# Second layer's heads: transposes of two units in a row in every other step

## The chip, the cores and the metric

The kernel runs on one core of a Trainium2 chip. The time is the device time of one execution in microseconds (us), the median of several runs. One execution is also recorded by the hardware profiler, and the profile shows that one alone.

The engines of a core work side by side, each through its own list of instructions in order: TensorE (PE for matmuls, PEld for its weight loads), VectorE (DVE), ScalarE (ACT), GpSimd (POOL), and SyncE (SP), which issues most DMAs here. An instruction that needs another engine's result waits for a semaphore, and everything behind it on its engine waits too.

## What is computed

Two layers of a bidirectional encoder over 512 tokens of width 1024, in float32. The first layer mixes tokens by neighbourhood attention, the second by multi-head latent attention; after each comes a gated embedding and at the end an RMSNorm. The change is in the second layer's heads:

```python
def block_attention(q, k, v):
    ...
    def one(qblk):
        s = jnp.einsum('bqhd,bkhd->bhqk', qblk, k).astype(jnp.float32) * scale
        pr = jax.nn.softmax(s, axis=-1).astype(v.dtype)
        return jnp.einsum('bhqk,bkhd->bqhd', pr, v)
    o = lax.map(one, qb)
    ...

def mixer_mla(xn, w_in, q_norm, w_qb, kv_norm, w_kvb, w_out):
    ...
    o = block_attention(q, k, v)
    return (o.reshape(B, S, H * MLA_V) * jax.nn.silu(z)) @ w_out
```

There are 16 heads and 512 queries, so 4 blocks of 128 queries for each head. Queries and keys have 64 plain and 32 rotary columns, and are projected from low-rank vectors.

## The kernel before

A float32 operand is kept as two float32r tiles, hi and lo (hi a rounded copy, which ScalarE writes, lo the rest, which VectorE or GpSimd subtracts), and a product of two operands is three matmuls: hi by hi, lo by hi, hi by lo. Weights come in by DMA as `wraw`, and `load_w` (L83, L84) splits them into `wwhi` on ScalarE and `wwlo` on GpSimd, here in two pieces each. What TensorE leaves in PSUM is evacuated by `split` (L94 on ScalarE, L96 or L98 on VectorE).

`mla_heads` works on 64 **units**: unit u is query block u mod 4 of head u // 4. A unit goes through three functions:

- `score(u)`: three matmuls of 512 columns into a PSUM tile `ps_S` (there are two of them), then the softmax by rows: VectorE takes the maximum (mx, L844), ScalarE the exponential with its row sum (L846), VectorE the reciprocal (rc, L847), and GpSimd multiplies (L848). The result is the tile `ex`, of which there are four.
- `turn(u)`: four transposes of 128x128 on TensorE (L139) of `ex` into a PSUM tile `ps_T` (there are three), which `split` evacuates to the head's tiles `pt_hi` (ScalarE, L94) and `pt_lo` (VectorE, L96).
- `output(h, s)`: for a whole head, four matmuls with `pt_hi` (s = 0) or `pt_lo` (s = 1) into the one PSUM tile `ps_O` (L863). Then `half_of` takes the result out (L204, L205), and after every second head `gated` multiplies by the gate and splits (L209 and L213 on GpSimd, L212 on ScalarE).

Beside them run the `pieces`: projections of the next heads' queries, keys and values (L751, L107), cut into parts over eight steps, with their weight loads. In every second group of eight steps a `rope` piece ends: ScalarE copies it (L784), VectorE shuffles and multiplies (L785, L786), GpSimd multiplies by the sine and adds (L787, L788), ScalarE and GpSimd split it (L789, L790). In steps 48 to 67 TensorE also works on pieces of the embedding (`ple`).

A loop of 70 steps lays this out. Step i holds, in this order, `score(i)`, the pieces of that step, a `turn`, and in steps with i mod 4 of 0 or 1 an `output` of the head two before. `turn` lags by three steps: unit i - 3 in step i. Each function is issued after the last matmul so far (`issue_after`), so TensorE's order is that of the loop. On the other engines a scheduler sets the order when the program is built, from its own modelled timeline; so a change of the loop changes the order of ScalarE, VectorE and GpSimd as well, though the loop says nothing of them.

Of the kernel before, what the change touches and what calls it, by code (L numbers as in the profile page):

```python
# [40 lines left out]
class Trunk:  # L41
# [692 lines left out]
    def mla_heads(self, pool, xT, cT, sets, oT):  # L734
# [98 lines left out]
        def score(i):  # L833
            h, qt = i // 4, i % 4
            st = sets[h // 2 % 2]
            q, k, kk = ((st["qe"], st["ke"], 96), (st["qo"], st["ko"], 128))[h % 2]
            if qt == 0:
                ST[h] = [self.small.tile([P, 4], F32, name=n, tag=n) for n in ("mx", "sm", "rc")]
            mx, sm, rc = (t[:, qt:qt + 1] for t in ST[h])
            sp = self.psum("S")  # L840
            Q = lambda s: q[s][0:kk, qt * P:(qt + 1) * P]
            K = lambda s: k[s][0:kk, :]
            self.mms(sp, [(Q(0), K(0)), (Q(0), K(1)), (Q(1), K(0))])
            nc.vector.reduce_max(mx, sp, axis=AX.X, negate=True)  # L844
            ex = EX[i] = pool.tile([P, S], F32, name="ex", tag="ex", bufs=4)
            nc.scalar.activation(ex, sp, AF.Exp, bias=mx, accum_out=sm)  # L846
            nc.vector.reciprocal(rc, sm)  # L847
            nc.gpsimd.tensor_tensor(out=ex, in0=ex, in1=rc.to_broadcast([P, S]), op=ALU.mult)  # L848

        def turn(i):  # L850
            h, qt = i // 4, i % 4
            if qt == 0:
                PT[h] = self.bigtile("pt_hi"), self.bigtile("pt_lo")
            ex = EX.pop(i)
            t = self.transposes([ex[:, n * P:(n + 1) * P] for n in range(4)])
            self.split(*(x[:, :, qt * P:(qt + 1) * P] for x in PT[h]), t.rearrange("p (a b) -> p a b", a=4))

        def output(h, s):
            if s == 0:
                PS["o", h] = self.psum("O")  # L860
            O = PS["o", h]
            for kt in range(4):
                self.last_mm = nc.tensor.matmul(O, V[h // 4][kt][:, h % 4 * P:(h % 4 + 1) * P], PT[h][s][:, kt, :],  # L863
                                                start=s == 0 and kt == 0, stop=s == 1 and kt == 3)
            if s == 0:
                return
            j, e = h // 2, h % 2
            if e == 0:
                U[j] = pool.tile([P, S], F32, name="u", tag="u", bufs=2)
            self.half_of(U[j], O, e)  # L870
            if e == 1:
                self.gated(U[j], zs[j], oT, j)

        def pieces(j):

            n, g = j + 1, j // 2 + 1
            w = [[] for i in range(8)]
            add = lambda i, f, *x: w[i].append(lambda: f(*x))
            if j == 0:
                add(0, queries, n, 0, 4)  # L880
                add(1, queries, n, 4, 9)
                add(2, keys, n, 0, 5)
                add(3, keys, n, 5, 6)
                for t in range(NT):
                    add((3, 4, 4, 5)[t], values, 0, t, "OOTT"[t])
            elif j < 7:
                add(0, queries, n, 0, 1)
                add(1, queries, n, 1, 3)
                add(2, queries, n, 3, 9)
                add(3, keys, n, 0, 4)  # L890
                add(4, keys, n, 4, 6)
            if j % 2 == 0 and j < 6:
                add(4, load_qn, g, ("k", n))
                add(5, rope, g, 0, 1)
                add(6, rope, g, 1, 5)
                add(7, rope, g, 5, 9)
                add(7, load_kv, g, ("r", g))
            elif j == 6:
                add(4, load, "w0", a["proj"][1, 0], 1024, ("q", n))
                add(6, ple)  # L900
                add(7, ple)
            elif j < 7:
                add(2, *((load_qr, g + 1, ("q", n), ("rl", g)) if j < 5 else
                         (load, "p", a["pT"][1], 1024, ("q", n), ("rl", g))))
                for t in range(NT):
                    add(6 + t // 2, values, g, t)
            else:
                add(0, load, "w1", a["proj"][1, 1], 1024, "latest")
                for i in (0, 1, 2, 3, 3, 4, 5, 6, 7, 7):
                    add(i, ple)  # L910
            return w
# [32 lines left out]
        for i in range(70):  # L944
            work = []
            if i < 64:
                work.append(lambda: score(i))
                work += pieces(i // 8)[i % 8]
            elif i < 68:
                work.append(ple)  # L950
            if 3 <= i < 67:
                work.append(lambda: turn(i - 3))
            if i >= 8 and i % 4 < 2:
                work.append(lambda: output(i // 4 - 2, i % 4))
            for f in work:
                with self.tc.issue_after(self.last_mm.ins):
                    f()
            if i == 53:
                last = self.last_mm
# [296 lines left out]
```

## Time and profile before

| what | value |
|---|---|
| median of 3 runs | 657.49 us (657.40 to 657.52) |
| the profiled execution's own time | 657.71 us |
| its span, first to last instruction | 655.6 us |
| second layer's heads, the loop | from about 406 to 562 us in the span |
| TensorE clock granted, mean | 0.997 |

In the profile a row of the timeline gives start and duration in us, engine, line, operation, `out<-in` by tile names, shapes, and how many instructions in a row it merges; brackets tell how long the engine was idle before and what released it. Starts of matmuls are sharp; their ends are modelled, and the pipeline overlaps them, so their cost is read from one start to the next. A row of the windows view gives, for one stretch of time, its length and the busy time of each engine with the number of instructions, then the granted clock, the share of DMA and GB/s.

### The profile page before, as it was taken

The page shows a single profiled execution, that of the slowest core. Times are in us where ns is not written, and L with a number is a line of the kernel's source. Part 1 is how long each engine was busy: PE and PEld are TensorE (multiplying, and loading weights), DVE is VectorE, ACT ScalarE, POOL GpSimd, SP SyncE. Part 2 cuts the span into 40 slices and gives each one's busy share as a digit, 9 for nine tenths or more (in the row PEclk, how much of TensorE's full clock was granted, in tenths as well). Part 3 has the DMA queues.
Part 4 walks back from the last instruction along what each step waited for, and adds up shares of the span by engine and source line. Part 5 has one row for each costly group of instructions (what it writes and reads, how often), then busy time and mean ns, then how long its engine had stood idle before and what let it go on. Part 6 is the DMA issues. An engine that isn't in the chain of part 4 may idle for free.

```text
span 655.6 us, 10131 instructions
## 1 busy us (share of the span) xinstructions
PE 645.4 (98%) x3419; PEld 551.1 (84%) x3419; DVE 398.9 (61%) x854; ACT 441.6 (67%) x879; POOL 433.3 (66%) x383
## 2 busy tenths in 40 slices
PE   9999999999999999999999999999999999999994
PEld 6888888998988888888899888888888888888884
DVE  6290365845646526569825613888888886464665
ACT  7672586766767743788743635887979897537855
POOL 0495475895685674697664626785969887437974
PEclk9999999999999999999999999999999999999998
DMA  9944254996575889535743344120111223673524
GB/s 324 353 140 150 94 198 123 252 226 153 206 162 195 191 177 364 168 131 166 242 123 108 104 99 150 48 76 7 63 53 66 66 70 124 224 289 129 191 66 160
DMA packets 44756, 102.18 MB, mean 156 GB/s; under 512 B 4640, under 2 KB 17696, under 8 KB 44704
## 3 DMA queue, kind: packets, MB, share of 16 engines
q1 hardware_dynamic: 33776, 83.97, 38.3%
q0 software_dynamic: 10496, 16.78, 11.8%
q10 hardware_dynamic: 432, 0.79, 0.3%
q8 instruction: 27, 0.44, 0.3%
q14 instruction: 25, 0.20, 0.1%
HBM read 89.99 MB, written 25.17 MB: 176 GB/s over the span
## 4 chain that ended last, share of the span: by engine, by line
PE 97%; ACT 1%; DMA 0%; DVE 0%; issue 0%; POOLq 0%; POOL 0%
PE ps_mm L107 35%; PE ps_S L107 12%; PE ps_mm L751 7%; PE ps_T L139 6%; PE ps_T L643 5%; PE ps_O L863 5%; PE ps_mm L643 3%; PE ps_S L643 3%; PE ps_T L107 3%; PE ps_T L238 2%; PE ps_O L400 2%; PE ps_O L107 2%; PE ps_mm L701 2%; PE ps_mm L184 2%; PE ps_T L388 2%; PE ps_S L701 1%
## 5 line engine op out<-in xcount | busy, mean ns | idle before, releaser
L84 POOL TENSOR_TENSOR wwlo<-wraw,wwhi 128x1024 fp32r<-128x1024 f32 (+5 forms) x78 | 142.9, 1846 | 75.5 <-ACT wwhi L83 54.0
L83 ACT ACTIVATE wwhi<-wraw 128x1024 fp32r<-128x1024 f32 (+5 forms) x81 | 65.5, 832 | 60.0 <-issue 18.0
L588 POOL TENSOR_TENSOR wlo<-wraw,whi 128x512 fp32r<-128x512 f32 x56 | 73.6, 1345 | 24.6 <-ACT whi L586 18.5
L848 POOL TENSOR_TENSOR ex<-ex,rc 128x512 f32<-128x512 f32 x64 | 66.2, 1043 | 26.0 <-DVE rc L847 22.0
L846 ACT ACTIVATE ex<-ps_S,mx 128x512 f32<-128x512 f32 x64 | 44.0, 687 | 11.8 <-DVE mx L844 10.1
L844 DVE TENSOR_REDUCE mx<-ps_S 128x1 f32<-128x512 f32 x64 | 43.7, 683 | 8.3 <-PE ps_S L107 7.9
L96 DVE TENSOR_TENSOR pt_lo<-ps_T,pt_hi 128x512 fp32r<-128x512 f32 x64 | 43.1, 681 | 7.1 <-ACT pt_hi L94 6.7
L374 POOL TENSOR_TENSOR ex<-ex,rc 128x128 f32<-128x128 f32 (+1 forms) x64 | 36.0, 617 | 15.0 <-DVE rc L370 15.0
L107 PE MATMUL ps_mm<-xh,wwhi 128*128 128x512 f32 x152 | 40.3, 398 | 0.0
L94 ACT ACTIVATE pt_hi<-ps_T 128x512 fp32r<-128x512 f32 x64 | 37.7, 594 | 3.4 <-PE ps_T L139 3.0
L107 PE MATMUL ps_mm<-xl,wwhi 128*128 128x512 f32 x152 | 38.5, 391 | 0.0
L139 PE MATMUL ps_T<-ident,ex 128*128 128x128 f32 x256 | 38.3, 272 | 0.0
L107 PE MATMUL ps_mm<-xh,wwlo 128*128 128x512 f32 x152 | 38.3, 392 | 0.0
L139 PEld LDWEIGHTS ps_T<-ident,ex 128*128 128x128 f32 x256 | 31.5, 140 | 7.5
L107 PEld LDWEIGHTS ps_mm<-xh,wwlo 128*128 128x128 f32 x152 | 28.3, 188 | 6.0
L586 ACT ACTIVATE whi<-wraw 128x1024 fp32r<-128x1024 f32 x28 | 29.2, 1054 | 6.0 <-DMA wraw<-sum 3.1
L107 PEld LDWEIGHTS ps_mm<-xl,wwhi 128*128 128x128 f32 x152 | 28.3, 188 | 5.7
L205 DVE TENSOR_TENSOR u<-ps_O,u 64x512 f32<-64x512 f32 x32 | 22.0, 686 | 17.2 <-ACT u L204 16.7
L368 ACT ACTIVATE ex<-ex,mx 128x128 f32<-128x128 f32 (+1 forms) x64 | 30.3, 475 | 2.6 <-DVE mx L358 1.8
L107 PEld LDWEIGHTS ps_mm<-xh,wwhi 128*128 128x128 f32 x152 | 27.3, 188 | 4.8
L209 POOL TENSOR_TENSOR u<-u,z 128x512 f32<-128x512 f32 x16 | 21.8, 1365 | 13.6 <-DVE u L205 8.3
L107 PE MATMUL ps_S<-ko,qo 128*128 128x512 f32 x96 | 28.9, 409 | 0.0
(441 smaller groups left out, 1848.7 us busy)
## 6 DMA issues: line engine op xcount, KB each, us to landing
sum<-gate POOLq DMA_DIRECT2D x12, 1024.0 KB, 7.7
wraw<-na_qk SPq DMA_DIRECT2D x16, 512.0 KB, 3.3
wraw<-sum SPq DMA_DIRECT2D x16, 512.0 KB, 3.3
pe<-pe SPq DMA_DIRECT2D x31, 256.0 KB, 7.0
wraw<-gate SPq DMA_DIRECT2D x12, 512.0 KB, 3.4
wraw<-na_v SPq DMA_DIRECT2D x8, 512.0 KB, 4.3
sum<-sum POOLq DMA_DIRECT2D x4, 1024.0 KB, 10.9
wraw<-na_o SPq DMA_DIRECT2D x8, 512.0 KB, 5.4
```

The source lines that it names most:

```text
L83: nc.scalar.activation(hi[:, c], raw[:, c], AF.Copy)
L84: f = lambda e, c=c: e.tensor_tensor(out=lo[:, c], in0=raw[:, c], in1=hi[:, c].bitcast(F32), op=ALU.subtract)
L94: self.last_copy = nc.scalar.activation(hi, src, AF.Copy, scale=scale)
L96: nc.vector.tensor_tensor(out=lo, in0=src, in1=hi.bitcast(F32), op=ALU.subtract)
L107: last = self.last_mm = nc.tensor.matmul(out, l, r, start=i == 0, stop=i == n - 1)
L139: self.last_mm = self.nc.tensor.transpose(t[:, i * P:(i + 1) * P], b, self.ident)
L588: nc.gpsimd.tensor_tensor(out=lo[:, o], in0=raw[:, o], in1=hi[:, o].bitcast(F32), op=ALU.subtract)
L643: mm = nc.tensor.matmul(ps, l, r, start=j == 0 and p in banks, stop=j == 11 and p in (2, 3, 4), skip_group_check=True)
L751: self.last_mm = nc.tensor.matmul(PS[key], *terms[i], start=i == 0, stop=i == len(terms) - 1)
L844: nc.vector.reduce_max(mx, sp, axis=AX.X, negate=True)
L846: nc.scalar.activation(ex, sp, AF.Exp, bias=mx, accum_out=sm)
L848: nc.gpsimd.tensor_tensor(out=ex, in0=ex, in1=rc.to_broadcast([P, S]), op=ALU.mult)
```

## The change

In `mla_heads`, `turn` no longer runs once in each step. In odd steps it runs twice, for units i - 3 and i - 2; in even steps from 4 on it does not run. So even units are transposed in step u + 3, as before, and odd units in step u + 2.

```diff
@@ -948,8 +948,8 @@
                 work += pieces(i // 8)[i % 8]
             elif i < 68:
                 work.append(ple)
-            if 3 <= i < 67:
-                work.append(lambda: turn(i - 3))
+            if i % 2 and 3 <= i < 67:
+                work += [lambda: turn(i - 3), lambda: turn(i - 2)]
             if i >= 8 and i % 4 < 2:
                 work.append(lambda: output(i // 4 - 2, i % 4))
             for f in work:
```

The instructions are the same ones; their order on the engines is not. TensorE from the transposes of unit 20 (step 23) to the output half of step 24, before:

```order
L139 MATMUL ps_T<-ident,ex 128x128 x4
L107 MATMUL ps_S<-ke_3538,qe_3534 128x512
L107 MATMUL ps_S<-ke_3539,qe_3534 128x512
L107 MATMUL ps_S<-ke_3538,qe_3535 128x512
L751 MATMUL ps_mm<-cT_3524,wwhi 128x512
L139 MATMUL ps_T<-ident,ex 128x128 x4
L863 MATMUL ps_O<-pt_hi,vt 128x512 x4
```

and with the change:

```order
L139 MATMUL ps_T<-ident,ex 128x128 x8
L107 MATMUL ps_S<-ke_3538,qe_3534 128x512
L107 MATMUL ps_S<-ke_3539,qe_3534 128x512
L107 MATMUL ps_S<-ke_3538,qe_3535 128x512
L751 MATMUL ps_mm<-cT_3524,wwhi 128x512
L863 MATMUL ps_O<-pt_hi,vt 128x512 x4
```

Unit 21's four transposes have moved ahead of the score of step 24 (the three ps_S rows), so that eight run in a row. Unit 23's move in the same way from step 26 to step 25, right behind those of unit 22.

GpSimd in the same stretch, before. The first row (two weight pieces) comes right behind the products of units 16 to 20; of the L848 rows, the first is unit 21, the next two are units 22 and 23, the last two 24 and 25:

```order
L84 TENSOR_TENSOR wwlo<-wraw,wwhi 128x384 x2
L848 TENSOR_TENSOR ex<-ex,rc 128x512
L209 TENSOR_TENSOR u<-u,z 128x512
L848 TENSOR_TENSOR ex<-ex,rc 128x512 x2
L84 TENSOR_TENSOR wwlo<-wraw,wwhi 128x512 x2
L787 TENSOR_TENSOR rl<-rl,rope_s 128x512
L213 TENSOR_TENSOR o1l_3980<-u,o1h_3978 128x512
L848 TENSOR_TENSOR ex<-ex,rc 128x512 x2
```

and with the change:

```order
L84 TENSOR_TENSOR wwlo<-wraw,wwhi 128x384 x2
L848 TENSOR_TENSOR ex<-ex,rc 128x512
L209 TENSOR_TENSOR u<-u,z 128x512
L848 TENSOR_TENSOR ex<-ex,rc 128x512
L84 TENSOR_TENSOR wwlo<-wraw,wwhi 128x512
L787 TENSOR_TENSOR rl<-rl,rope_s 128x512
L84 TENSOR_TENSOR wwlo<-wraw,wwhi 128x512
L848 TENSOR_TENSOR ex<-ex,rc 128x512
L213 TENSOR_TENSOR o1l_3980<-u,o1h_3978 128x512
L788 TENSOR_TENSOR rl<-rh,rl 128x512
L848 TENSOR_TENSOR ex<-ex,rc 128x512 x2
```

Unit 23's product, which stood right behind unit 22's, now stands behind two weight pieces and the first rope product. The same rows come again sixteen units later, for units 37 to 41.

ScalarE in the same stretch, before (L846 are the exponentials of units 21, 22 and 23, `pt_hi` the evacuations of units 18, 19 and 20):

```order
L83 ACTIVATE wwhi<-wraw 128x384 x2
L94 ACTIVATE pt_hi<-ps_T 128x4x128
L846 ACTIVATE ex,sm<-ps_S,mx 128x512
L204 ACTIVATE u<-ps_O 64x512
L846 ACTIVATE ex,sm<-ps_S,mx 128x512
L94 ACTIVATE pt_hi<-ps_T 128x4x128
L846 ACTIVATE ex,sm<-ps_S,mx 128x512
L784 ACTIVATE rh<-ps_mm 128x512
L83 ACTIVATE wwhi<-wraw 128x512 x2
L94 ACTIVATE pt_hi<-ps_T 128x4x128
```

and with the change (`pt_hi` of units 18 and 19, exponentials of units 21, 22 and 23):

```order
L94 ACTIVATE pt_hi<-ps_T 128x4x128
L94 ACTIVATE ko_3540<-ps_mm 64x512
L83 ACTIVATE wwhi<-wraw 128x384 x2
L94 ACTIVATE pt_hi<-ps_T 128x4x128
L846 ACTIVATE ex,sm<-ps_S,mx 128x512
L204 ACTIVATE u<-ps_O 64x512
L846 ACTIVATE ex,sm<-ps_S,mx 128x512
L784 ACTIVATE rh<-ps_mm 128x512
L83 ACTIVATE wwhi<-wraw 128x512 x2
L846 ACTIVATE ex,sm<-ps_S,mx 128x512
```

Both evacuations now stand ahead of the exponential of unit 21, and the exponential of unit 23 has gone behind the copy of the rope projection and two weight pieces.

## The prediction

> **What bounds the kernel now.** I read the busy shares first, then the time by stage, then the chain of waits, then the timeline of each engine around one place. A unit is one block of 128 queries of one head of the second layer, numbered 0 to 63; unit u is scored in step u of the loop.
>
> ```profile
> span 655.6 us, 10131 instructions
> PE 645.4 (98%) x3419; PEld 551.1 (84%) x3419; DVE 398.9 (61%) x854; ACT 441.6 (67%) x879; POOL 433.3 (66%) x383
> PE 97%; ACT 1%; DMA 0%; DVE 0%; issue 0%; POOLq 0%; POOL 0%
> core 0: us, PE busy (x) PEld busy (x) DVE busy (x) ACT busy (x) POOL busy (x), PEclk, DMA share, GB/s
> 400.00:562.00 162.00, 162.00 (x884) 136.41 (x883) 129.37 (x258) 136.35 (x297) 124.68 (x116) 1.00 0.22 67
> ```
>
> TensorE is 97% of the chain, and in the 162 us that hold the second layer's heads it is busy in every one of them at clock 1.00. The loop has no TensorE wait that a change could remove: it can gain only by cheaper TensorE work, and whatever makes TensorE wait there is paid in full. The other three are not idle either: VectorE 129, ScalarE 136 and GpSimd 125 of 162 us.
>
> **TensorE's own work.** The rows from step 23 to step 25 (ps_S with three matmuls is a score, ps_T four transposes, ps_O an output half):
>
> ```profile
> 457.20 0.95 PE L107 MATMUL ps_S<-ko,qo 128*128 128x512 f32 x3
> 457.98 0.39 PE L751 MATMUL ps_mm<-cT,wwhi 128*128 128x512 f32 x1
> 458.21 0.86 PE L751 MATMUL ps_mm<-cT,wwlo 128*128 128x512 f32 x3
> 458.91 0.60 PE L139 MATMUL ps_T<-ident,ex 128*128 128x128 f32 x4
> 459.26 0.94 PE L107 MATMUL ps_S<-ke,qe 96*128 96x512 f32 x3
> 460.04 0.39 PE L751 MATMUL ps_mm<-cT,wwhi 128*128 128x512 f32 x1
> 460.27 0.60 PE L139 MATMUL ps_T<-ident,ex 128*128 128x128 f32 x4
> 460.63 1.18 PE L863 MATMUL ps_O<-pt_hi,vt 128*128 128x512 f32 x4
> 461.64 0.86 PE L107 MATMUL ps_S<-ke,qe 96*128 96x512 f32 x3
> 462.35 0.62 PE L751 MATMUL ps_mm<-cT,wwhi 128*128 128x512 f32 x2
> 462.81 0.60 PE L139 MATMUL ps_T<-ident,ex 128*128 128x128 f32 x4
> 463.16 1.17 PE L863 MATMUL ps_O<-pt_lo,vt 128*128 128x512 f32 x4
> 464.17 0.62 PE L107 MATMUL ps_S<-ke,qe 96*128 96x512 f32 x2
> ```
>
> Starts tell the cost, since matmuls are pipelined. A score that follows no transposes takes 462.35 - 461.64 = 0.71, one that follows four takes 460.04 - 459.26 = 0.78, and four transposes take 459.26 - 458.91 = 0.35. So a block of four moves everything behind it by 0.35 + 0.07 = 0.42 (I use 0.43, from the ps_O rows: 464.17 - 463.16 = 1.01 against four at 0.23). The change keeps all 64 blocks. Is the 0.07 to 0.08 a price of going from transposes back to matmuls, which 32 longer blocks would pay half as often, or the tail of the last transpose? Between nothing and 32 x 0.08 = 2.6 us can be saved. I take nothing: 0.43 is 0.11 for each of four, and the group's row spreads four starts of 0.27 us over 0.60, which is (0.60 - 0.27) / 3 = 0.11 each; the 0.08 is what the fourth still lacks.
>
> **What the move asks of the others.** An odd unit's transposes went in step u + 3; now they go in step u + 2, right behind those of unit u - 1. Their operand ex must be there earlier: it comes from VectorE's maximum, ScalarE's exponential, VectorE's reciprocal and GpSimd's product, in each engine's own order. For unit 23 this is:
>
> ```profile
> 453.86 0.60 PE L139 MATMUL ps_T<-ident,ex 128*128 128x128 f32 x4
> 454.25 0.94 ACT L83 ACTIVATE wwhi<-wraw 128x384 fp32r<-128x384 f32 x2
> 455.71 0.68 ACT L846 ACTIVATE ex<-ps_S,mx 128x512 f32<-128x512 f32 x1
> 456.51 0.59 ACT L204 ACTIVATE u<-ps_O 64x512 f32<-64x512 f32 x1
> 458.18 0.69 DVE L844 TENSOR_REDUCE mx<-ps_S 128x1 f32<-128x512 f32 x1 [0.25 <-PE ps_S L107]
> 458.35 1.29 POOL L209 TENSOR_TENSOR u<-u,z 128x512 f32<-128x512 f32 x1
> 459.60 2.04 POOL L848 TENSOR_TENSOR ex<-ex,rc 128x512 f32<-128x512 f32 x2
> 461.59 2.55 POOL L84 TENSOR_TENSOR wwlo<-wraw,wwhi 128x512 fp32r<-128x512 f32 x2
> 464.10 1.30 POOL L787 TENSOR_TENSOR rl<-rl,rope_s 128x512 f32<-128x512 f32 x1
> 465.34 1.31 POOL L213 TENSOR_TENSOR o1l<-u,o1h 128x512 fp32r<-128x512 f32 x1
> ```
>
> The two products from 459.60 are units 22 and 23; the second ends at 459.60 + 2.04 = 461.64. Unit 22 is transposed at 462.81 and unit 23 a step later. GpSimd then works without a pause on two weight pieces, a rope product and a gated output. The new program has another order here: on GpSimd unit 23 stands behind weight piece, rope product and weight piece, instead of ahead of them. And on TensorE it is now wanted right behind unit 22, at 462.81 + 0.43 = 463.24. (Step 25 begins where it did: the odd block of step 24 has gone to step 23, and both lie ahead of it.)
>
> **Lower bound of this wait.** Let all that comes before be as in these rows. GpSimd takes up the first weight piece when unit 22 is done, at 459.60 + 1.00 = 460.60; the two pieces take 464.10 - 461.59 = 2.51, the rope product 465.34 - 464.10 = 1.24, the product of unit 23 1.04: it ends at 465.39. TensorE waits 465.39 - 463.24 = 2.15 us. Its rope operand is no excuse for less: the rope matmuls end with the start of the transposes at 458.91, and ScalarE's copy and VectorE's shuffle need less than the 3 us until GpSimd gets there.
>
> **Upper bound.** The new order also makes the engines ahead of unit 23 later. On ScalarE a second evacuation of transposes (that of unit 19, 0.5) stands ahead of the exponential of unit 21, which the row has at 455.71 to 456.39; the score of unit 22 begins 0.43 later, since unit 19's block is now ahead of it, and with it VectorE's maximum of unit 22. Going along the new orders with these durations: unit 18's transposes, which do not move, begin at 453.86, so ScalarE evacuates them from 454.35 on; a key half (0.5) and the two weight pieces (0.94) follow, then the new evacuation of unit 19, 456.4 to 456.9, and only then the exponential of unit 21, 456.9 to 457.6. On VectorE its reciprocal now stands behind the maximum of unit 22 and the second half of unit 19's evacuation, 0.65 each from 456.9 on: 458.25. GpSimd gets unit 21 at 458.5, its gate product at 459.5, unit 22 at 460.75 to 461.75, against an end at 460.60 in the rows. Two pieces, rope product and unit 23 follow: 461.75 + 2.51 + 1.24 + 1.04 = 466.54. Against 463.24 that is 3.3 us (about 0.4 of it already as a wait of score 23 for the buffer that exponential 21 frees, since it is due at 457.20). I take 2.9, nearer the upper end, since the walk has the whole new order and the lower bound assumes none of it.
>
> **The same place again.** Sixteen units later the same orders stand:
>
> ```profile
> 497.04 2.05 POOL L848 TENSOR_TENSOR ex<-ex,rc 128x512 f32<-128x512 f32 x2
> 499.04 2.56 POOL L84 TENSOR_TENSOR wwlo<-wraw,wwhi 128x512 fp32r<-128x512 f32 x2
> 501.54 1.30 POOL L787 TENSOR_TENSOR rl<-rl,rope_s 128x512 f32<-128x512 f32 x1
> 502.78 1.30 POOL L213 TENSOR_TENSOR o1l<-u,o1h 128x512 fp32r<-128x512 f32 x1
> 500.26 0.60 PE L139 MATMUL ps_T<-ident,ex 128*128 128x128 f32 x4
> ```
>
> Unit 38 ends on GpSimd at 498.04; 2.50 + 1.24 + 1.05 put unit 39 at 502.83 against 500.26 + 0.43 = 500.69: 2.14 again. The first place of this kind, around unit 7, has the product of unit 7 still ahead of the weight pieces, and units 8 and 9, which come after them, are wanted only two steps later: no wait.
>
> **The rest of the loop.** Most odd units have room for one step. The tightest are in the last stretch, where TensorE does little between scores:
>
> ```profile
> 532.51 1.04 POOL L848 TENSOR_TENSOR ex<-ex,rc 128x512 f32<-128x512 f32 x1 [1.19 <-DVE rc L847]
> 537.02 1.04 POOL L848 TENSOR_TENSOR ex<-ex,rc 128x512 f32<-128x512 f32 x1
> 533.15 0.60 PE L139 MATMUL ps_T<-ident,ex 128*128 128x128 f32 x4
> 537.75 0.60 PE L139 MATMUL ps_T<-ident,ex 128*128 128x128 f32 x4
> ```
>
> Unit 53 ends at 533.55 and is now due at 533.15 + 0.43 = 533.58; unit 55 ends at 538.06 and is due at 538.18. Any delay of theirs is a wait. In the new order the reciprocal of unit 53 stands behind two evacuations and a maximum of the next unit. I put 0.4 for each of the two, with bounds 0 and 1: 0.7 us together after rounding down.
>
> Nothing else costs or gives time back: no instruction and no DMA is added or dropped; the outputs have their pt tiles a step sooner, but did not wait for them; and SP's queue changes the place of a few moves and loads in stretches where the DMA share is 0.22.
>
> **Sum.** 2 x 2.9 + 0.7 = 6.5 us on the profiled span of 655.6: 662.1. The execution itself took 657.71, 2.1 more than its span; the median of the runs shown is 657.49, so 1.9 lies around the span. 655.6 + 6.5 + 1.9 = **664.0 us**. With the lower bounds 2 x 2.15 = 4.3: 661.8. With the upper ones 2 x 3.3 + 2 = 8.6: 666.1.
>
> [...] The rows first, for the end of the program, where TensorE has nothing left to do:
>
> ```profile
> 646.45 0.40 PE L643 MATMUL ps_O<-wlo,X 128*128 128x256 f32 x2
> 650.00:652.00 2.00, 0.00 (x0) 0.00 (x0) 0.91 (x2) 0.72 (x1) 0.56 (x1) 1.00 0.60 225
> 652.00:654.00 2.00, 0.00 (x0) 0.00 (x0) 0.00 (x0) 0.00 (x0) 0.00 (x0) 0.50 0.83 303
> ```
>
> TensorE's last matmul ends at 646.85, and the granted clock stays 1.00 until about 652, 5 us later, before it is 0.50. Two waits of 3 us are shorter, so I give the clock no price. [...]
>
> **Rivals.**
> - *The transposes get cheaper in longer blocks* and nothing waits: 657.5 - 2.6 = 654.9. For it: the 0.08 behind each block. Against: that 0.08 is explained by four equal transposes, and unit 23's place in the queue stays. It would decide only if the price of going back were over 0.2 us for each of the 32 blocks, which no row leaves room for.
> - *The waits are hidden*: GpSimd gets to unit 23 in time, as it would if rope and weights were ready sooner and its queue ran ahead. 657.5. Against: unit 22 itself comes only at 459.60, and 4.8 us of work then stand before the end of unit 23.
> - *The clock falls* in each of the two waits. Step 25 takes 464.17 - 461.64 = 2.5 us, and would take 2.5 more at half clock: 664.0 + 2 x 2.5 = 669.0.
> - *The waits spread*: two blocks in a row give ScalarE and VectorE two evacuations together, and exponentials come half a microsecond late in most pairs. With 0.3 us in a dozen of the 32 pairs on top of the sum: 664.0 + 3.6 = 667.6.
>
> **How the numbers follow.** The two waits on GpSimd 0.75; spread waits 0.10; clock 0.05; hidden 0.07; cheaper transposes 0.03. The time is that of the first, 664.0. The range takes its bounds, a little below 661.8 and up to the spread case: 660.8 to 667.6. A measurement tells 0.2%, 1.3 us, from no change; all cases of waiting lie beyond it, so slower has 0.89 (0.75 + 0.10 + 0.05, less 0.01 for waits that shrink), same 0.08, faster 0.03.
>
> **What would show it.** In the new trace: TensorE idle before L139 in two places, some 2 to 3 us each, at the blocks of units 22/23 and 38/39, released by GpSimd's ex at L848; GpSimd without a pause ahead of it; the four-transpose spacing unchanged, eight taking 0.78 to 0.79 from first start to the next matmul; TensorE busy in the loop without these gaps for the same 162 us. It is wrong if TensorE does not wait for unit 23, if it waits mainly for ScalarE's exponential or the ps_S buffers, or if blocks of eight take less than 0.75.

## The result, and the profile after

The changed kernel takes 666.81 us (median of 4 runs, 666.34 to 667.12), the kernel before on the same chip 657.44 us (657.28 to 657.52). The ratio is 1.014, with a 95% interval of 1.0127 to 1.0153: 9.4 us slower. The forecast was 664.0 us, in a range of 660.8 to 667.6. The profiled execution spans 665.0 us, against 655.6 before.

The page of the changed kernel, and the windows view of its loop:

```profile
span 665.0 us, 10121 instructions
PE 648.6 (98%) x3419; PEld 553.2 (83%) x3419; DVE 397.8 (60%) x854; ACT 441.7 (66%) x879; POOL 433.2 (65%) x383
PE 88%; DVE 4%; POOL 3%; ACT 2%; issue 1%; DMA 0%; POOLq 0%; ACTq 0%; DVEq 0%
400.00:572.00 172.00, 165.87 (x887) 138.86 (x886) 129.00 (x257) 136.46 (x296) 124.78 (x115) 0.99 0.21 64
```

TensorE still has its 3419 matmuls and is busy 98% of the span, but the chain that ended last now runs over the other engines for a tenth of it. In the loop TensorE is idle for 172.00 - 165.87 = 6.1 us, where it was never idle before; the work that VectorE, ScalarE and GpSimd are given is the same. What TensorE waited for there, from the view of waits (total, times, longest):

```profile
PE ps_T L139 <- POOL ex L848: 4.4, 2, 2.2
PE ps_S L107 <- ACT ex L846: 1.5, 3, 0.6
```

The first row is the pair of long waits, at units 23 and 39. TensorE's timeline around the first:

```profile
453.42 1.03 PE L139 MATMUL ps_T<-ident,ex 128*128 128x128 f32 x8
454.21 1.17 PE L863 MATMUL ps_O<-pt_lo,vt 128*128 128x512 f32 x4
455.22 0.85 PE L107 MATMUL ps_S<-ko,qo 128*128 128x512 f32 x3
455.91 1.07 PE L751 MATMUL ps_mm<-cT,wwhi 128*128 128x512 f32 x4
457.58 0.96 PE L107 MATMUL ps_S<-ko,qo 128*128 128x512 f32 x3 [0.60 <-ACT ex L846]
...
463.19 0.60 PE L139 MATMUL ps_T<-ident,ex 128*128 128x128 f32 x4
466.00 0.66 PE L139 MATMUL ps_T<-ident,ex 128*128 128x128 f32 x4 [2.22 <-POOL ex L848]
466.41 0.94 PE L863 MATMUL ps_O<-pt_lo,vt 128*128 128x512 f32 x3
```

Three things are read here. Units 18 and 19, which did not wait, take 454.21 - 453.42 = 0.79 us for eight transposes, and the output half behind them 455.22 - 454.21 = 1.01. The score of unit 23 begins 457.58 - 455.91 = 1.67 after four matmuls of 0.93, so it waits 0.74, until ScalarE's exponential of unit 21 frees the ps_S buffer. And units 22 and 23 take 466.41 - 463.19 = 3.22 instead of 0.79: a wait of 2.43. (The bracket says 2.22, as it counts from the modelled end of the transpose ahead.) What GpSimd does meanwhile:

```profile
460.18 1.04 POOL L848 TENSOR_TENSOR ex<-ex,rc 128x512 f32<-128x512 f32 x1
461.18 1.29 POOL L84 TENSOR_TENSOR wwlo<-wraw,wwhi 128x512 fp32r<-128x512 f32 x1
462.44 1.28 POOL L787 TENSOR_TENSOR rl<-rl,rope_s 128x512 f32<-128x512 f32 x1
463.69 1.26 POOL L84 TENSOR_TENSOR wwlo<-wraw,wwhi 128x512 fp32r<-128x512 f32 x1
464.92 1.03 POOL L848 TENSOR_TENSOR ex<-ex,rc 128x512 f32<-128x512 f32 x1
```

Unit 22, a weight piece, the rope product, the other weight piece, unit 23, with no pause between them. Unit 23 ends at 465.95, and TensorE goes on at 466.00.

Behind the second long wait, from 507.64 on, stands something that has no counterpart at the first:

```profile
507.64 0.66 PE L139 MATMUL ps_T<-ident,ex 128*128 128x128 f32 x4 [2.22 <-POOL ex L848]
508.06 1.17 PE L863 MATMUL ps_O<-pt_lo,vt 128*128 128x512 f32 x4
509.06 1.44 PE L107 MATMUL ps_S<-ke,qe 96*128 96x512 f32 x3
510.30 1.48 PE L751 MATMUL ps_mm<-cT,wwhi 128*128 128x512 f32 x3
511.58 1.29 PE L751 MATMUL ps_mm<-cT,wwlo 128*128 128x512 f32 x3
512.70 0.86 PE L107 MATMUL ps_S<-ke,qe 96*128 96x512 f32 x3
```

The score from 509.06 takes 1.24, where 0.71 is usual, and the six matmuls from 510.30 take 512.70 - 510.30 = 2.40 instead of 1.39. The granted clock is 0.50 from 509.10 to 512.51, against 1.00 before and behind it: 1.54 us more.

### The profile page after: what moved, and what is told of

It reads as the page before. It is cut to its first block, busy times and chain, and to the rows that moved or that the text cites. A ratio compares the mean times of both kernels' runs of the same rounds, so it can differ in the third digit from the quotient of the medians.

```text
span 665.0 us, 10121 instructions
## 1 busy us (share of the span) xinstructions
PE 648.6 (98%) x3419; PEld 553.2 (83%) x3419; DVE 397.8 (60%) x854; ACT 441.7 (66%) x879; POOL 433.2 (65%) x383
## 4 chain that ended last, share of the span: by engine, by line
PE 88%; DVE 4%; POOL 3%; ACT 2%; issue 1%; DMA 0%; POOLq 0%; ACTq 0%; DVEq 0%
PE ps_mm L107 34%; PE ps_S L107 10%; PE ps_T L643 5%; PE ps_T L139 5%; PE ps_mm L751 5%; PE ps_mm L643 3%; PE ps_O L863 3%; PE ps_S L643 3%; PE ps_T L107 2%; PE ps_T L238 2%; PE ps_O L400 2%; PE ps_O L107 2%; PE ps_mm L701 2%; PE ps_mm L184 2%; PE ps_T L388 2%; DVE mx L844 1%
## 5 line engine op out<-in xcount | busy, mean ns | idle before, releaser
L848 POOL TENSOR_TENSOR ex<-ex,rc 128x512 f32<-128x512 f32 x64 | 66.0, 1041 | 33.3 <-DVE rc L847 20.1
L846 ACT ACTIVATE ex<-ps_S,mx 128x512 f32<-128x512 f32 x64 | 44.0, 687 | 14.1 <-DVE mx L844 12.5
L139 PE MATMUL ps_T<-ident,ex 128*128 128x128 f32 x256 | 34.2, 273 | 4.6 <-POOL ex L848 4.4
L139 PEld LDWEIGHTS ps_T<-ident,ex 128*128 128x128 f32 x256 | 29.7, 140 | 9.2 <-POOL ex L848 5.6
```

What stands on the lines that cost most here:

```text
L139: self.last_mm = self.nc.tensor.transpose(t[:, i * P:(i + 1) * P], b, self.ident)
```

## The experiments

Units 23 and 39 are one place each, sixteen units apart. The waits found at one came at the other within 0.1 us, but for the run without pairs; the slow clock did not. The theory was that GpSimd's queue is too full there for the earlier deadline of unit 23, and that running two units in a row costs TensorE nothing in itself. The rivals were that pairs burden ScalarE and VectorE in bursts, that only the order of GpSimd's queue is at fault, and that the clock makes up most of the loss. The first four runs were timed beside the kernel before at 657.64 us, the next four at 657.48, the last three at 657.60.

### One cost taken away: two subtractions on GpSimd

```diff
             f = lambda e, c=c: e.tensor_tensor(out=lo[:, c], in0=raw[:, c], in1=hi[:, c].bitcast(F32), op=ALU.subtract)
-            if late is not None and c.stop == n:
+            if self.bydma:
+                self.move(lo[:, c], hi[:, c])
+            elif late is not None and c.stop == n:
...
         def load_kv(g, after=None):
+            self.bydma = g > 1
             load(("kv", g), a["mla_kv"][g], 1024, after)
+            self.bydma = False
```

> The change, but GpSimd does not make the lo pieces of the two key/value weight loads that stand ahead of units 23 and 39; a DMA copies hi into lo instead, so the subtraction is left out (the result is not the reference's). Theory (GpSimd's queue is full there, and the earlier deadline of unit 23 and 39 meets it): the two 2.4 us waits before the transposes of units 23 and 39 shrink to under 0.4 us each and the slow-clock stretch after the second goes too; the waits of about 0.9 us before the scores of units 23 and 39 and the small ones of units 53 and 55 stay: 660 us (659.4 to 661.2). Rival (two blocks in a row burden ScalarE and VectorE, and GpSimd only inherits their delay): waits of over 1.5 us stay at those transposes: 664 or more. Rival (the blocks of eight cost TensorE itself): 665 or more.

At each of the two places GpSimd is spared two subtractions; a DMA copies hi into lo in their stead, so this kernel's output is not the reference's. It takes 659.14 us, a ratio to the kernel before of 1.0026 (1.0018 to 1.0035). In its profile TensorE no longer waits for GpSimd at units 23 or 39 at all; what it waits for is

```profile
PE ps_S L110 <- ACT ex L851: 1.2, 2, 0.6
```

the two scores, and small waits of 0.23 and 0.28 at units 53 and 55. So the long waits are the price of 2.5 us of GpSimd work ahead of unit 23. Without them the slow clock is gone too: the mean granted clock is 0.996 or 0.997 in all eleven runs, where it was 0.993 in all four of the change. The time came out just under the expected range.

### Units 23 and 39 alone go back a step

```diff
             if i % 2 and 3 <= i < 67:
-                work += [lambda: turn(i - 3), lambda: turn(i - 2)]
+                work.append(lambda: turn(i - 3))
+                if i not in (25, 41):
+                    work.append(lambda: turn(i - 2))
+            elif i in (26, 42):
+                work.append(lambda: turn(i - 3))
```

> The change, but the transposes of units 23 and 39 alone stay a step later, as before; GpSimd's order stays that of the change. Theory: those two waits vanish, units 24 and 25 (40 and 41) are then late by about 0.3 and 0.6 us, the score waits stay: 661.5 us (660 to 663). Rival (bursts in all 32 pairs): 30 pairs stay, so over 665.

661.83 us, ratio 1.0066 (1.0052 to 1.0079): as expected. 30 of 32 pairs stay, GpSimd's order up to unit 23 is that of the change, and over half of the loss is gone, 1.5 us of it the slow clock, which this run does not have: its mean granted clock is 0.996 or 0.997 in all five executions. What is left at this place, besides the score:

```profile
469.76 0.66 PE L139 MATMUL ps_T<-ident,ex 128*128 128x128 f32 x4 [0.69 <-POOL ex L848]
470.76 0.65 PE L139 MATMUL ps_T<-ident,ex 128*128 128x128 f32 x4 [0.34 <-POOL ex L848]
```

Units 24 and 25 now wait: GpSimd is still behind when they are due.

### GpSimd's order of before

```diff
-            nc.gpsimd.tensor_tensor(out=ex, in0=ex, in1=rc.to_broadcast([P, S]), op=ALU.mult)
+            A["ex"] = nc.gpsimd.tensor_tensor(out=ex, in0=ex, in1=rc.to_broadcast([P, S]), op=ALU.mult)
...
-            (nc.gpsimd if g else nc.vector).tensor_tensor(out=sw, in0=sw, in1=rs_t, op=ALU.mult)
+            with self.tc.issue_after(A["ex"].ins) if g else nullcontext():
+                (nc.gpsimd if g else nc.vector).tensor_tensor(out=sw, in0=sw, in1=rs_t, op=ALU.mult)
...
-                add(7, load_kv, g, ("r", g))
+                add(7, load_kv, g, ("r", g), "ex")
```

(`load_kv` hands the last name to `load`, which queues the weight pieces behind that product.)

> The change, with GpSimd made to take units 23 and 39 ahead of the two weight pieces and the rope product, as before. If the order of the queue alone were the cause, the two waits go: 660. If GpSimd's work in that stretch as a whole is what does not fit the earlier deadlines, the wait moves on to units 24 and 25, 0.4 and 1.9 us at each of the two places: 665 to 666.5, about as slow as the change. I expect the second.

665.31 us, ratio 1.0122 (1.0108 to 1.0136). Unit 23 is in time, and the wait has moved on whole:

```profile
463.48 1.12 PE L139 MATMUL ps_T<-ident,ex 128*128 128x128 f32 x8
...
469.94 0.66 PE L139 MATMUL ps_T<-ident,ex 128*128 128x128 f32 x4 [0.69 <-POOL ex L849]
472.17 0.66 PE L139 MATMUL ps_T<-ident,ex 128*128 128x128 f32 x4 [1.58 <-POOL ex L849]
```

Units 22 and 23 go through as eight; 24 and 25 wait 0.85 and 1.74 by their starts. The order alone is not the cause.

### GpSimd's and ScalarE's orders

To the run before are added: the rope copy behind the step's exponential on ScalarE, and the evacuations of steps 21 and 37 behind theirs.

```diff
+            with self.tc.issue_after(A["exp"].ins) if g else nullcontext():
+                A["r", g] = nc.scalar.activation(xr, psr, AF.Copy)
...
+                    with self.tc.issue_after(A["exp"].ins) if i in (21, 37) else nullcontext():
+                        turn(i - 3)
+                        turn(i - 2)
```

> The change, with GpSimd taking units 23 and 39 first, and ScalarE taking the exponentials ahead of the rope copy and, in steps 21 and 37, ahead of the two evacuations. Theory: the score waits (0.9 each) go, unit 23 is ready earlier, GpSimd's stretch begins a microsecond earlier, and what is left are waits of some 0.6 us at units 24 and 25 at each place and those of units 53 and 55: 659.3 us (658.3 to 661). Rival (pairs as such cost): 664 or more.

661.89 us, ratio 1.0064 (1.0051 to 1.0076), above the expected range: the score waits are gone, but units 23, 24 and 25 still wait 0.46, 0.91 and 0.51 by their starts, more than I had walked out.

### The changed kernel again

> The changed kernel once more, to see its clock. If the slow stretch behind the second long wait is set by where a wait falls in a fixed window of time, its place may differ: behind the first, the second, both or none, 1.5 us each; the waits themselves stay at 2.2 to 2.5 us. If it is set by the length of the wait alone, both waits (of one length) should bring the same, which one trace has already against it.

665.45 us, in one run. The waits are the same (4.4 us in two, 1.5 in three), and the clock stays up behind both: its mean is 0.997, where it was 0.993 in each of the four runs behind the median of 666.81. So the 1.5 us of slow clock is there in most executions and not in all; it is no fixed part of the change.

### Every unit a step earlier, no pairs

```diff
-            if i % 2 and 3 <= i < 67:
-                work += [lambda: turn(i - 3), lambda: turn(i - 2)]
+            if 2 <= i < 66:
+                work.append(lambda: turn(i - 2))
```

> No pairs: each step transposes one unit, but every unit a step earlier than before (unit i - 2 in step i). Theory (the earlier deadline costs, not the pair): TensorE waits for GpSimd's products at units 24 to 26 and 40 to 42 (together 1.5 to 2 us at each place) and in the stretch of units 45 to 58 (1 to 3 us): 661 to 666. Rival (the pair is what costs): no waits, 657.5.

668.82 us, ratio 1.0172 (1.0157 to 1.0187), beyond the expected range on the slow side. TensorE waits for GpSimd's ex nine times, 7.6 us in all, and for nothing else. The longest, of 3.4 us at unit 43, is behind a rope half and two weight pieces:

```profile
513.32 1.30 POOL L790 TENSOR_TENSOR rl<-rl,rh 128x512 fp32r<-128x512 f32 x1 [1.36 <-ACT rh L789]
514.58 2.49 POOL L84 TENSOR_TENSOR wwlo<-wraw,wwhi 128x512 fp32r<-128x512 f32 x2
517.03 3.04 POOL L848 TENSOR_TENSOR ex<-ex,rc 128x512 f32<-128x512 f32 x3
```

No pair is left in this kernel, and it loses more than the change, so an earlier step is enough to make TensorE wait. The comparison goes no further: even units are a step earlier here too, and GpSimd's order is another again. Unit 23, due in the same step as in the change, does not wait, since GpSimd takes it ahead of the two weight pieces, and unit 43, which did not wait in the change, waits longest.

### ScalarE's order alone

The second half of the diff of the fourth run, without the rest.

> The change, with ScalarE made to take the exponentials of units 21 and 37 ahead of the two evacuations of those steps. Theory: the score waits of 0.9 us at units 23 and 39 go, but units 23 and 39 are still behind the weight pieces and the rope product, which start at most 0.5 us sooner, so the waits at their transposes become 2.4 to 2.9 us: 664.5 to 666. Rival (ScalarE's order is the root of both waits): both go, 660 or less.

669.14 us, ratio 1.0178 (1.0161 to 1.0195): beyond the expected range, and worse than the change. The scores of units 23 and 39 no longer wait, but the scheduler, given this order, put a weight piece ahead of unit 22 on GpSimd as well; the transposes of unit 22 wait 0.40, those of unit 23 2.95, the score of unit 25 0.60, and the slow clock is there behind the second place (0.50 from 509.94 to 513.35). I had the direction and not the size. As ScalarE's order, held right, does not bring unit 23 forward, it is not the root of both waits.

### The weight load two steps earlier

```diff
-                add(7, load_kv, g, ("r", g))
...
+                add(5, load_kv, g, ("k", n))
```

> The change, with the key/value weight load two steps earlier (in step 21, 37 instead of 23, 39), so that GpSimd does those pieces before units 21 and 37. GpSimd is busy from about 456 us on there, so if its whole work is the limit, unit 21 is late instead (1 to 1.6 us) and unit 23 by less (0.7): 662 to 666. If only the place of the pieces in its queue matters: 660.

665.58 us, ratio 1.0122 (1.0107 to 1.0137), in the expected range, though by another wait: four weight pieces now stand ahead of the exponential of unit 21 on ScalarE, and the score of unit 23 waits 1.8 us for it, units 21 and 23 another 0.63 and 0.55. Together 3.0 us at the place, as in the change (0.74 + 2.43 = 3.2). At the first place of this kind, which did not wait in the change, the score of unit 7 now waits 0.52 and unit 5 0.35. Two steps moved the wait to another engine; they did not take it out of the stretch.

### Pairs only where there is room

```diff
             if i % 2 and 3 <= i < 67:
-                work += [lambda: turn(i - 3), lambda: turn(i - 2)]
+                work.append(lambda: turn(i - 3))
+                if i - 2 not in single:
+                    work.append(lambda: turn(i - 2))
+            elif i - 3 in single:
+                work.append(lambda: turn(i - 3))
```

where `single` holds the odd units 19 to 29, 35 to 45 and 51 to 57.

> The change where units had room only: pairs stay for units 0 to 18, 30 to 34, 46 to 50 and 58 to 63 (16 of 32 pairs), and the odd units 19 to 29, 35 to 45 and 51 to 57 go a step later, as before. Theory (a pair costs and saves TensorE nothing; only missed deadlines cost): no TensorE wait in the loop of over 0.3 us, 657.5 us (657.0 to 658.3). Rival (each pair costs, by bursts on ScalarE and VectorE): half of the change's loss stays, 661 or more. Rival (a block of eight is cheaper for TensorE than two of four, hidden so far under the waits): 656.5 or less.

659.74 us, ratio 1.0034 (1.0022 to 1.0046): slower than expected. No wait for GpSimd's ex of 0.2 us or more is left, but three for ScalarE, 1.7 us together. ScalarE's timeline shows why:

```profile
454.29 0.60 ACT L94 ACTIVATE pt_hi<-ps_T 128x512 fp32r<-128x512 f32 x1 [0.81 <-PE ps_T L139]
454.91 0.60 ACT L94 ACTIVATE ko<-ps_mm 64x512 fp32r<-64x512 f32 x1
455.53 0.94 ACT L83 ACTIVATE wwhi<-wraw 128x384 fp32r<-128x384 f32 x2
456.50 0.59 ACT L204 ACTIVATE u<-ps_O 64x512 f32<-64x512 f32 x1
457.11 0.69 ACT L846 ACTIVATE ex<-ps_S,mx 128x512 f32<-128x512 f32 x1
```

It sits 0.81 us before the evacuation of unit 18, whose transposes are not done yet, with a key half and two weight pieces behind it that in the kernel before ran from 453.63 on. So the exponential of unit 21, at 455.71 in the kernel before, comes at 457.11. The order was made for a modelled timeline. At this place the loop is that of the kernel before, and the pairs further up were enough to change ScalarE's order here.

### The same, with ScalarE's order held

```diff
+            for f in late:
+                with self.tc.issue_after(self.last_mm.ins):
+                    with self.tc.issue_after(A["exp"].ins) if i in range(16, 58) else nullcontext():
+                        f()
```

(`late` holds the step's `turn` and `output`; a second version does this in steps 21 and 37 alone.)

> The 16 pairs with room of the run before, and in steps 16 to 57 ScalarE takes the step's exponential ahead of that step's evacuations. Theory (what the 16 pairs still cost was ScalarE's new order, which put an evacuation that TensorE had not yet produced ahead of the exponentials of units 21 and 37): the two score waits of 0.85 us and the one of 0.5 go, GpSimd has unit 23 ready at about 465.4 for transposes at 466.2, no wait over 0.3 us is left: 657.6 us (657.2 to 658.4). Rival (pairs as such cost 0.1 us each or more, wherever): 659 or more.

> The same with ScalarE's order held in steps 21 and 37 only; there GpSimd takes unit 23 behind the two weight pieces, the rope product and the gated output. Theory: the score waits go; unit 23 ends at about 466.7 for transposes due at 466.2, so a wait of 0.3 to 0.7 us at each of the two places: 658.6 us (657.9 to 659.4).

The first takes 658.27 us, ratio 1.0014 (1.0005 to 1.0022): within 0.2% of the kernel before by its median, with 16 pairs in it. One wait of size is left, a new kind, 0.9 us by the starts:

```profile
520.79 0.63 PE L139 MATMUL ps_T<-ident,ex 128*128 128x128 f32 x4 [0.75 <-DVE pt_lo L96]
```

The second half of a pair waits for one of the three ps_T buffers, which VectorE has not yet emptied, since the evacuations now stand behind the exponentials. The second version, 659.93 us (1.0022 to 1.0049), lies above its expected range. It keeps waits of about half a microsecond at scores 25 and 41 and at units 23 and 39; those of the scores I had not expected.

No version beat the kernel before. TensorE has no idle time in the loop there, so an order that takes none of its work away has nothing to gain; that is read from the profile, and these runs don't speak against it.

## Why the prediction was right, and where it was short

**Blocks of eight save nothing: right.** 0.79 for eight and 1.01 for the four matmuls behind them, where two blocks of four took 0.35 each with 1.01 behind each. Two times 0.35 plus 0.08 for what the fourth still lacks is 0.78.

**The waits at units 23 and 39: right in place, cause and engine; the size was at the upper bound.** 2.9 us each was taken, the score's wait included, between 2.15 and 3.3. Measured: 0.74 + 0.1 at the score (its three matmuls took 0.80 behind the wait, where 0.71 is usual) and 2.43 at the transposes, 3.3 in all. The walk along the new orders put the exponential of unit 21 at 456.9, and it ran at 456.76:

```profile
456.26 0.60 ACT L94 ACTIVATE pt_hi<-ps_T 128x512 fp32r<-128x512 f32 x1
456.76 0.68 ACT L846 ACTIVATE ex<-ps_S,mx 128x512 f32<-128x512 f32 x1
```

These two times are not on one clock, though: unit 18's transposes, from which the walk counts, begin at 453.42 here and at 453.86 in the rows it was worked out from. Counted from them, the walk had the exponential at 3.04 and it came at 3.34, since ScalarE began unit 18's evacuation 0.15 later than the walk has it and took 0.62, not 0.5, for it and for the key half behind it. So the score waited 0.84 and not about 0.4. The end of unit 23, 12.68 by the walk, came at 12.53. The split between the two waits was off, and their sum was right. The upper bound was the walk itself, and should have been the value.

**Units 53 and 55: right.** 0.29 and 0.35 by the starts of the matmuls behind them, 0.64 together, for a forecast of 0.7. As forecast, the reciprocal of unit 53 came behind two evacuations and a maximum on VectorE, and GpSimd's product ended at 542.34 for transposes that went on at 542.40. Unit 55's product stood behind a weight piece, which the forecast did not have.

**What was not seen: a wait at the score of unit 30, 0.6 us.** It is 0.44 before that score and some 0.1 each for the slow first matmuls of units 30 and 31. In the changed order ScalarE's rope copy `rh` (L789) stands ahead of the output's evacuation, and waits for GpSimd's L788. That holds up VectorE's maximum of unit 26:

```profile
468.48 0.63 ACT L789 ACTIVATE rh<-rl 128x512 fp32r<-128x512 f32 x1 [1.19 <-POOL rl L788]
469.13 0.59 ACT L204 ACTIVATE u<-ps_O 64x512 f32<-64x512 f32 x1
469.83 0.68 DVE L205 TENSOR_TENSOR u<-ps_O,u 64x512 f32<-64x512 f32 x1 [1.81 <-ACT u L204]
470.44 0.67 DVE L844 TENSOR_REDUCE mx<-ps_S 128x1 f32<-128x512 f32 x1
```

The score of unit 26 was at 467.43, so its maximum comes 2 us later than it could; the exponentials behind it stay late until the score of unit 30 stands still for its buffer, which the exponential of unit 28 frees. The link from the one to the other is read from the timeline, not tried; the first four runs have no such wait.

**The clock: the rival that was given 0.05 came in part.** The forecast put no price on the clock, since 5 us of idle time at the program's end had left it at 1.00; the rival had 2.5 us behind each of the two waits. In the profiled execution it fell to 0.50 behind one of them, which cost 1.5 us, and behind none in another execution. The 5 us were misread as a limit: in the changed kernel a wait of 2.2 us was followed by 0.50. Cut as in the last section, the 5 us lay across two stretches: the first, with TensorE busy for 1.67 us, was followed by 1.00, and the second, with 0.00, by 0.50.

**The sum.** 2 x 3.3 + 0.64 + 0.64 + 1.5 = 9.4, which is the difference of the spans, 665.0 - 655.6. That it agrees to the tenth is partly luck: the changed kernel began the score of unit 21 at 452.51, 0.43 before the kernel before, and small delays elsewhere used that up. The forecast of 6.5 lacks 0.7 at the two places, 0.6 at unit 30 and 1.5 of clock. That 666.8 still lies in the range is luck as well: by the upper bounds of its own terms the forecast ended at 666.1, and the room above that was left for waits spread over many pairs, which did not come. Of the rivals, the cheaper transposes and the hidden waits are out by the profile, and waits spread over all pairs are out by the second run, with 30 pairs and less than half of the loss, and by one more: the last run but one has 16 pairs, where there is room, at a ratio of 1.0014 (1.0005 to 1.0022), with its one wait of size accounted for.

## What to carry to other kernels

Where one engine is busy without a gap, do not ask what a reordering saves on it, but what it makes due earlier, and walk the queue of each engine that delivers: the price is the work that stands ahead of the needed result, less the room it had. When the order of the other engines comes from a scheduler's model, a change of one loop line changes queues far from it; read the new queues before trusting the old ones, and take the walk's own result, not a mean with the case in which nothing else moves. A wait that goes away at one unit may only move to the next, as long as the engine behind it is full (with GpSimd's order of before, units 24 and 25 waited 0.85 and 1.74 us in place of unit 23): take work away from that engine, or leave the deadline.

## What the hardware showed that was not expected

In the changed kernel two waits of TensorE of one length, 2.22 us each by the brackets, were followed by different clocks: 1.00 behind the first, and behind the second 0.50 for 3.41 us. In its trace the granted clock falls at 509.10, rises at 512.51, 3.41 us later, and falls again at 659.28, at the end of the program. From the rise to that last fall it is 146.77 us, and 146.77 / 43 = 3.41. So the traces are cut here into stretches of 3.41 us, counted from such a fall. In the windows view a row has the stretch and its length, then the busy us of TensorE's matmuls and weight loads, VectorE, ScalarE and GpSimd, the granted clock, the DMA share and GB/s. Windows of the changed kernel:

```profile
464.73:468.14 3.41, 2.14 (x12) 1.83 (x13) 1.33 (x3) 1.03 (x3) 3.41 (x4) 1.00 0.51 159
505.69:509.10 3.41, 1.46 (x9) 1.29 (x10) 1.24 (x5) 1.71 (x4) 3.41 (x4) 1.00 0.38 124
509.10:512.51 3.41, 3.41 (x10) 2.64 (x9) 2.00 (x4) 2.00 (x4) 3.41 (x4) 0.50 0.17 52
512.51:515.92 3.41, 3.41 (x21) 2.89 (x20) 1.71 (x4) 2.16 (x5) 2.27 (x3) 1.00 0.28 67
```

Of the same kernel's repetition, at about the same place (the clock stays at 1.00 there, so no fall marks where to cut):

```profile
505.84:509.25 3.41, 1.57 (x9) 1.40 (x10) 1.27 (x5) 1.64 (x4) 3.41 (x4) 1.00 0.43 131
509.25:512.66 3.41, 3.41 (x17) 2.74 (x16) 2.20 (x5) 2.49 (x5) 3.41 (x4) 1.00 0.17 49
```

Of the run with ScalarE's order alone:

```profile
506.53:509.94 3.41, 0.62 (x6) 0.39 (x5) 1.01 (x4) 1.27 (x3) 3.41 (x4) 1.00 0.39 129
509.94:513.35 3.41, 3.41 (x11) 2.75 (x10) 0.96 (x2) 1.19 (x2) 3.41 (x4) 0.50 0.08 30
```

Of the run without pairs:

```profile
514.62:518.03 3.41, 0.10 (x1) 0.00 (x0) 2.54 (x6) 2.11 (x6) 3.41 (x5) 1.00 0.44 104
518.03:521.44 3.41, 3.32 (x10) 2.83 (x11) 0.69 (x1) 1.06 (x2) 2.04 (x3) 0.50 0.42 154
```

And of the kernel before, at the end of the program, where the clock falls at 652.01:

```profile
645.18:648.59 3.41, 1.67 (x14) 1.46 (x13) 3.27 (x9) 3.17 (x10) 0.55 (x1) 1.00 0.64 241
648.59:652.00 3.41, 0.00 (x0) 0.00 (x0) 2.12 (x5) 1.57 (x4) 1.54 (x2) 1.00 0.53 198
```

Each slow stretch shown in the loop is 3.41 us long. It follows a stretch of 3.41 us in which TensorE was busy for 1.46, 0.62 and 0.10 us. Where it was busy for 1.57 at the same place of the repetition, the clock stayed at 1.00, and so it did in the changed kernel behind the first wait, which lay across two such stretches, with TensorE busy for 2.46 and 2.14. The program's end in the kernel before fits: the stretch with the last matmuls, busy for 1.67, was followed by 1.00 and the empty one behind it by 0.50, so the 5 us say nothing of how short a wait can be. In the traces of the kernel before and of the change, cut in this way from end to end, every stretch in which TensorE was busy for 1.46 us or less was followed by a clock of 0.50 (leaving out the last of each, with no full stretch behind it in the span), and every one in which it was busy for 1.67 or more by 1.00. Nothing between 1.46 and 1.57 was tried, and nothing here shows where the limit lies.
